# Meta scores by two matmuls a block instead of three, in a hybrid attention encoder on one core

## The chip, the cores and the metric

The kernel runs on one core of a Trainium2 chip. The metric is the device time of one execution in microseconds (us), lower is better. Inside the core five engines run side by side, each through its own instruction list in order: TensorE (PE in the profile, with PEld for its weight loads), VectorE (DVE), ScalarE (ACT), GpSimd (POOL) and SyncE (SP), which here issues all the DMA transfers. TensorE reads its operands from SBUF, the on-chip memory of 128 partitions, and writes to PSUM, a smaller memory that VectorE and ScalarE read.

## The reference

One encoder layer is applied to two token groups, 1024 prompt tokens and 256 sample tokens; each has 16 learned meta tokens put ahead of it. Cut to what matters:

```
u = rms_norm(h, norm_w) @ w_in                    # 2048 -> 6656, 52 strips of 128 columns
qa, ka, va, za, qb, kb, vb, zb = split(u)
# A heads (8, sharing 2 key/value heads): every query sees 16 meta keys and all real keys
s = q . k * 128**-0.5 ;  p = softmax(s) ;  o = p . v
# B heads (8): every query sees 16 meta keys and an 8x16 window of real keys, plus a position bias
s_meta = q . k_meta * scale
s_win  = q . k_win * scale + bias
p = softmax(concat(s_meta, s_win)) ; o = p_meta . v_meta + p_win . v_win
y = concat(o_a * silu(za), o_b * silu(zb)) @ w_out
return h + y                                       # real tokens only
```

All data is float32. The scores are large enough (the norm gains are scaled by 8) that the kernel keeps more than one rounded product: it splits an operand into a high part, rounded to the matmul's fast float32 kind (`F32R` in the code), and a low part, the rest, and sums high x high, high x low and low x high in PSUM. A plain float32 matmul needs no split and stands as two passes in the trace.

## The kernel before, in words

Tokens are processed in two chunks. Chunk 1 (0 to about 580 us) holds the sample tokens, the meta tokens and the first 240 prompt tokens; chunk 2 (to about 1800 us) the other 784 prompt tokens. In each chunk `strips` multiplies 128-column strips of `w_in` with the normalised tokens, 16 steps of three matmuls (L205 to L207) a strip and a block of up to 512 tokens. That stream of projection matmuls is most of the work of TensorE, and the attention blocks are laid between it. From about 1800 us on `outproj` (L946 to L948) makes the output.

An attention block covers 256 queries. There are 80 of them: 40 with all keys (`attend`; 8 sample blocks in chunk 1, 32 prompt blocks in chunk 2), 32 with windows (`attend_strip`, chunk 2 and the start of the output projection) and 8 sample blocks with windows (`attend_sample`, which makes its meta scores in one plain float32 matmul). A block runs: scores of the real keys (L328 to L330, or L434); scores of the meta keys; maximum over all keys (VectorE L278, then a reduction over partitions on GpSimd, L280); subtraction of it and exponentials; sums (L295, L297 on GpSimd); the product with the values (L368 to L370, or L466) and, in one more matmul, with the meta values (L371, L463); normalisation, gate and store (`put_y`).

The change concerns the meta scores of the 72 blocks of `attend` and `attend_strip`. The 16 meta keys stand three times side by side as 48 weight columns, so that the scores come out in three copies, on partitions 0 to 15, 16 to 31 and 32 to 47; `meta_probs` later turns the three into high, high and low parts of the probabilities (L285 to L290) for a single matmul with the meta values. `meta_scores` makes the scores with three matmuls of 256 query columns: high keys x high queries, high keys x low queries, low keys x high queries, all summed into the same 48 partitions of PSUM (L268 to L270); ScalarE then copies them, scaled, to the SBUF tile `Sm` (L272). The keys' tile `km` is built once per key head by `copy_km` (L500) or in `k_load` (L780, L781), and its two halves are handed on as a pair.

The order of the work is not written out. The kernel is traced in the order of the code, and a scheduler that carries estimated times lays out each engine's list. So an edit of one helper can move instructions far from it. SBUF is handed out by pools that are stacked one behind another: a tile that grows moves all that lie behind it. Each pool rotates a given number of buffers; `sp`, the PSUM pool of the scores, has two, `sm`, which holds `Sm`, has two.

Of the kernel before, what the change touches and what calls it, by code (L numbers as in the profile page):

```python
# [12 lines left out]
F32 = mybir.dt.float32  # L13
F32R = mybir.dt.float32r
AF = mybir.ActivationFunctionType
# [5 lines left out]
P = 128  # L21
DM = 2048
KT = 16
NMETA = 16
M3 = 3 * NMETA
NS = 256
NP = 1024
C1P = 240
# [10 lines left out]
QB = 256  # L39
# [11 lines left out]
class Kern:  # L51
# [212 lines left out]
    def meta_scores(self, pm, meta, qh, ql, scale):  # L264

        nc = self.nc
        kh, kl = meta
        nc.tensor.matmul(pm, kh, qh, start=True, stop=False)  # L268
        nc.tensor.matmul(pm, kh, ql, start=False, stop=False)
        nc.tensor.matmul(pm, kl, qh, start=False, stop=True)  # L270
        sm = self.sm.tile([M3, QB], F32, tag="Sm", name="Sm")
        nc.scalar.activation(sm[:], pm, AF.Copy, scale=scale)  # L272
        return sm

    def all_max(self, m1, sm):
# [41 lines left out]
    def attend(self, q, zs, keys, meta, vals, vmeta, ydst):  # L317

        nc = self.nc
        nt = len(keys)  # L320
        qh, ql = q[:, 0, :], q[:, 1, :]
        S = []
        mx = None
        for p in range(nt // 2):
            ps = self.sp.tile([P, 2, QB], F32, tag="sp", name="sp")
            for i in range(2):
                kh, kl = keys[2 * p + i]
                nc.tensor.matmul(ps[:, i, :], kh, qh, start=True, stop=False)  # L328
                nc.tensor.matmul(ps[:, i, :], kh, ql, start=False, stop=False)  # L329
                nc.tensor.matmul(ps[:, i, :], kl, qh, start=False, stop=True)  # L330
            s = self.s.tile([P, 2, QB], F32, tag="S", name="S")
            nc.scalar.copy(s[:], ps[:])  # L332
            S.append(s)
            if p == 1:
                mx = self.mx.tile([P, 2, QB], F32, tag="mx", name="mx")
                nc.vector.tensor_tensor(out=mx[:], in0=S[0][:], in1=ps[:], op=ALU.max)
            elif p > 1:
                nc.vector.tensor_tensor(out=mx[:], in0=mx[:], in1=ps[:], op=ALU.max)
        pm = self.sp.tile([P, 2, QB], F32, tag="sp", name="sm_ps")
        sm = self.meta_scores(pm[:M3, 0, :], meta, qh, ql, 1.0)  # L340
        src = S[0] if mx is None else mx
        m1 = self.t.tile([P, QB], F32, tag="t", name="m1")
        nc.vector.tensor_tensor(out=m1[:], in0=src[:, 0, :], in1=src[:, 1, :], op=ALU.max)
        ma = self.all_max(m1, sm)
        mb = ma[:].unsqueeze(1).to_broadcast([P, 2, QB])
        for p in range(nt // 2):
            s = S[p][:]
            nc.vector.tensor_tensor(out=s, in0=s, in1=mb, op=ALU.subtract)  # L348
            nc.scalar.activation(s, s, AF.Exp, scale=SCALE)
            if p == 1:  # L350
                acc = self.mx.tile([P, 2, QB], F32, tag="mx", name="acc")
                nc.vector.tensor_tensor(out=acc[:], in0=S[0][:], in1=S[1][:], op=ALU.add)
            elif p > 1:
                nc.vector.tensor_tensor(out=acc[:], in0=acc[:], in1=s, op=ALU.add)
        pm3 = self.meta_probs(sm, ma, SCALE)
        src = S[0] if nt == 2 else acc
        a1 = self.t.tile([P, QB], F32, tag="t", name="a1")
        nc.vector.tensor_tensor(out=a1[:], in0=src[:, 0, :], in1=src[:, 1, :], op=ALU.add)
        tot = self.all_sum(a1, sm)
        po = self.op.tile([P, QB], F32, tag="po", name="po")  # L360
        for j in range(nt):
            p, i = divmod(j, 2)
            if i == 0:
                ph = self.ph.tile([P, 2, QB], F32R, tag="ph", name="ph")
# [6 lines left out]
        nc.tensor.matmul(po[:], vmeta, pm3[:], start=False, stop=True)  # L371
        self.put_y(po, tot, zs, ydst)
# [39 lines left out]
    def attend_strip(self, q, qf, zs, k, meta, vals, vmeta, tab, w, ydst):  # L412

        nc = self.nc
        qv = q[:].rearrange("p i (g r) -> p i g r", g=4)[:, :, :, 64 * w:64 * w + 64]
        qfv = qf[:].rearrange("p (g r) -> p g r", g=4)[:, :, 64 * w:64 * w + 64]
        groups = {0: (0, 2), 3: (2, 4), 1: (0, 3), 2: (1, 4)}
        pa = self.sp.tile([P, 2, QB], F32, tag="sp", name="sp")  # L420
        pb = self.sp.tile([P, 2, QB], F32, tag="sp", name="sp")
        sa = self.s.tile([P, 2, QB], F32, tag="S", name="S")
        sb = self.s.tile([P, 2, QB], F32, tag="S", name="S")
        pa, pb, sa, sb = (x[:].rearrange("p a b -> p (a b)") for x in (pa, pb, sa, sb))

        def part(a, b, t):

            return (a[:, :P], b[:, :192], b[:, 192:384], a[:, P:2 * P])[t]

        for t in (0, 3, 1, 2):  # L430
            a, e = groups[t]
            dst = part(pa, pb, t)
            o = NMETA + 256 * t + 32 * WIN0[w]
            nc.tensor.matmul(dst, k[:, o:o + P], qfv[:, a:e, :], start=True, stop=True)  # L434
            if t == 3:
                sm = self.meta_scores(pa[:M3, 256:], meta, qv[:, 0], qv[:, 1], SCALE)
        ty = WTYPE[w]
        for x, y, n, o in ((sa, pa, 256, 64), (sb, pb, 384, 0)):
            nc.vector.scalar_tensor_tensor(out=x[:, :n], in0=y[:, :n], scalar=SCALE, in1=tab[:, ty, o:o + n],
                                           op0=ALU.mult, op1=ALU.add)  # L440
# [22 lines left out]
        nc.tensor.matmul(po[:], vmeta, pm3[:], start=True, stop=False)  # L463
        for t in (0, 3, 1, 2):
            a, e = groups[t]
            nc.tensor.matmul(po[:, 64 * a:64 * e], vals[:, t, :], part(sa, sb, t), start=False, stop=t == 2)  # L466
        self.put_y(po, tot, zs, ydst)
# [28 lines left out]

    def copy_km(self, k):

        km = self.k.tile([P, 2, 3, NMETA], F32R, tag="km", name="km")
        self.nc.scalar.copy(km[:], k.bitcast(F32).unsqueeze(2).to_broadcast([P, 2, 3, NMETA]))  # L500
        km = km[:].rearrange("p i c m -> p i (c m)")
        return km[:, 0], km[:, 1]

    def load_vm(self, g):

# [178 lines left out]
    def chunk2(self):  # L684
# [89 lines left out]
        def k_load(g):  # L774
            k = self.k.tile([P, NMETA + NP], F32, tag="k1", name="kfull")
            nc.sync.dma_start(k[:, :K0], self.kfd[g][:])
            nc.sync.dma_start(k[:, K0:], self.k2d[g][:])
            km = self.k.tile([P, 2, 3, NMETA], F32R, tag="km", name="km")
            full = k[:, :NMETA].unsqueeze(1).to_broadcast([P, 3, NMETA])
            nc.scalar.copy(km[:, 0], full)  # L780
            nc.vector.tensor_tensor(out=km[:, 1], in0=full, in1=km[:, 0].bitcast(F32), op=ALU.subtract)  # L781
            km = km[:].rearrange("p i c m -> p i (c m)")
            return k, (km[:, 0], km[:, 1])

        def q_load(h):
            qf = self.qf.tile([P, NP], F32, tag="qf", name="qfull")
# [416 lines left out]
```

## Time and profile before

| | |
|---|---|
| median of three runs | 2207.62 us (2204.06 to 2210.12) |
| the profiled execution | 2206.77 us, of which the span of the trace is 2204.7 us |
| TensorE busy in the span | 2180.8 us (99%), weight loads beside it 1964.3 us |
| VectorE, ScalarE, GpSimd busy | 1634.2, 1115.5 and 525.2 us |
| granted TensorE clock | 0.999 of full speed over the span |
| the 216 meta-score matmuls | 72 each on L268, L269 and L270 |

In the rows of the profile, a group reads: line, engine, operation, output tile <- input tiles, shape, count, then busy time and mean duration, then idle time of the engine before it and what ended it. A row such as `128*48 128x256` is a matmul with 48 weight columns and 256 streamed columns. Matmuls overlap in the pipeline, so the duration of one (280 ns) is longer than the distance from its start to the start of the next; the cost of one in a full stream is that distance. Times in a row of a waits view are us in total, number of times, longest.

### The profile page before, as it was taken

Reading aid. Unit: us, or ns where it says so; the run is one execution under the profiler, and the core shown is the slowest. Engines: PE = TensorE matmul, PEld = TensorE weight load, DVE = VectorE, ACT = ScalarE, POOL = GpSimd, SP = SyncE. Lnnn points to the kernel's source line nnn. Section 1 sums busy time; section 2 is a strip of 40 time slices with the busy share of each in tenths; the row PEclk is TensorE's granted clock in tenths of the full one; section 3 lists DMA queues with packets and bytes.
Section 4 is the critical chain, followed back from the end, with each engine's and each line's share of the span. In section 5 each row is a group of like instructions: output and inputs, shape, how many; then the busy total and the mean of one; then the engine's idle time right before and its main releaser. Section 6 shows DMA issues by size and latency. Waiting matters only on the chain.

```text
span 2204.7 us, 36270 instructions
## 1 busy us (share of the span) xinstructions
PE 2180.8 (99%) x12816; PEld 1964.3 (89%) x12816; DVE 1634.2 (74%) x2895; ACT 1115.5 (51%) x2272; POOL 525.2 (24%) x249
## 2 busy tenths in 40 slices
PE   8999999999999999999999999999999999999999
PEld 7888788888878999999999999998889889999999
DVE  7687876787764989976899989767768777536743
ACT  6555444455454666755666756444444454222220
POOL 1232421132211332221233223423423312000000
PEclk9999999999999999999999999999999999999999
DMA  8767889989464333334333335644433464745663
GB/s 291 224 191 226 268 287 309 331 271 291 135 214 146 107 111 115 102 110 142 101 107 111 105 121 161 184 144 133 126 114 115 136 225 151 234 136 163 212 205 112
DMA packets 264533, 383.96 MB, mean 174 GB/s; under 512 B 45824, under 2 KB 120224, under 8 KB 264352
## 3 DMA queue, kind: packets, MB, share of 16 engines
q1 hardware_dynamic: 264352, 381.66, 54.5%
q8 instruction: 100, 1.64, 0.3%
q14 instruction: 81, 0.66, 0.1%
HBM read 281.01 MB, written 100.38 MB: 173 GB/s over the span
## 4 chain that ended last, share of the span: by engine, by line
PE 89%; DVE 5%; DMA 3%; issue 1%; ACT 1%; POOL 0%; SPq 0%; DVEq 0%; POOLq 0%; ACTq 0%
PE pp L205 20%; PE pp L207 20%; PE pp L206 19%; PE pq L947 6%; PE pq L948 6%; PE pq L946 6%; PE po L466 2%; PE sp L330 1%; PE sp L328 1%; PE sp L329 1%; PE po L368 1%; PE po L369 1%; PE po L370 1%; PE sp L434 1%; DMA wr<-in_w_in 1%
## 5 line engine op out<-in xcount | busy, mean ns | idle before, releaser
L205 PE MATMUL pp<-x,wh 128*128 128x512 f32 (+1 forms) x2496 | 895.2, 360 | 8.7 <-ACT wh L57 7.2
L207 PE MATMUL pp<-x,wl 128*128 128x512 f32 (+1 forms) x2496 | 890.6, 357 | 0.0
L206 PE MATMUL pp<-x,wh 128*128 128x512 f32 (+1 forms) x2496 | 889.1, 356 | 0.2 <-DVE x L155 0.2
L205 PEld LDWEIGHTS pp<-x,wh 128*128 128x128 f32 x2496 | 469.2, 188 | 72.7 <-ACT wh L57 8.5
L206 PEld LDWEIGHTS pp<-x,wh 128*128 128x128 f32 x2496 | 470.5, 188 | 60.8 <-DVE x L155 0.9
L207 PEld LDWEIGHTS pp<-x,wl 128*128 128x128 f32 x2496 | 469.1, 188 | 61.9 <-DVE wl L58 0.7
L58 DVE TENSOR_TENSOR wl<-wr,wh 128x512 fp32r<-128x512 f32 (+1 forms) x402 | 303.8, 768 | 139.2 <-ACT wh L57 86.5
L57 ACT CAST wh<-wr 128x512 fp32r<-128x512 f32 (+1 forms) x402 | 240.1, 611 | 237.7 <-PE pp L206 169.3
L215 POOL PARTITION_ALL_REDUCE m<-ms x78 | 228.9, 2934 | 410.1 <-ACT ms L213 371.0
L297 POOL PARTITION_ALL_REDUCE tot<-a x80 | 178.8, 2234 | 454.6 <-DVE a L295 431.2
L947 PE MATMUL pq<-ym,wh 128*128 128x320 f32 x896 | 276.9, 309 | 1.9 <-DVE ym L58 1.9
L948 PE MATMUL pq<-ym,wl 128*128 128x320 f32 x896 | 276.8, 309 | 0.7 <-DVE wl L58 0.7
L946 PE MATMUL pq<-ym,wh 128*128 128x320 f32 x896 | 276.2, 309 | 1.1 <-ACT ym L57 1.1
L280 POOL PARTITION_ALL_REDUCE ma<-m x80 | 108.1, 1351 | 420.7 <-DVE m L278 417.1
L947 PEld LDWEIGHTS pq<-ym,wh 128*128 128x128 f32 x896 | 168.1, 188 | 2.6 <-DVE ym L58 2.6
L946 PEld LDWEIGHTS pq<-ym,wh 128*128 128x128 f32 x896 | 168.0, 188 | 1.7 <-ACT ym L57 1.7
L948 PEld LDWEIGHTS pq<-ym,wl 128*128 128x128 f32 x896 | 168.1, 188 | 1.0 <-DVE wl L58 0.9
L190 ACT CAST wh<-wr 128x512 fp32r<-128x512 f32 x132 | 81.6, 618 | 52.7 <-PE pp L206 49.6
L332 ACT COPY S<-sp 128x512 f32<-128x512 f32 x136 | 78.5, 582 | 56.3 <-PE sp L330 51.3
L64 ACT ACTIVATE rs_l<-m 128x512 f32<-128x512 f32 (+1 forms) x78 | 43.9, 563 | 124.1 <-DVE m L216 119.4
L348 DVE TENSOR_TENSOR S<-S,ma 128x512 f32<-128x512 f32 x136 | 98.4, 779 | 9.2 <-POOL ma L280 9.2
L58 DVE TENSOR_TENSOR pl<-S,ph 128x512 fp32r<-128x512 f32 x136 | 97.3, 727 | 9.9 <-ACT ph L57 9.2
(201 smaller groups left out, 3185.9 us busy)
## 6 DMA issues: line engine op xcount, KB each, us to landing
wr<-in_w_in SPq DMA_DIRECT2D x414, 256.0 KB, 3.8
wld<-wl SPq DMA_DIRECT2D x132, 256.0 KB, 4.6
wl<-wld SPq DMA_DIRECT2D x132, 256.0 KB, 3.3
wq<-in_w_out SPq DMA_DIRECT2D x64, 256.0 KB, 5.5
td<-wq SPq DMA_DIRECT2D x64, 256.0 KB, 4.6
wr<-td SPq DMA_DIRECT2D x64, 256.0 KB, 3.4
yr<-yd SPq DMA_DIRECT2D x48, 320.0 KB, 4.1
wr<-in_w_out SPq DMA_DIRECT2D x48, 256.0 KB, 3.8
```

The source lines that it names most:

```text
L57: self.hi = nc.scalar.copy(hi, full).ins
L58: return nc.vector.tensor_tensor(out=lo, in0=full, in1=hi.bitcast(F32), op=ALU.subtract).ins
L205: nc.tensor.matmul(p[:, :n], wh[:, k, :], xh[:, :n], start=first, stop=False)
L206: nc.tensor.matmul(p[:, :n], wh[:, k, :], xl[:, :n], start=False, stop=False)
L207: nc.tensor.matmul(p[:, :n], wl[:, k, :], xh[:, :n], start=False, stop=last)
L215: nc.gpsimd.partition_all_reduce(m2[:], ms[:], P, RED.add)
L280: nc.gpsimd.partition_all_reduce(ma[:], m1[:], P, RED.max)
L297: nc.gpsimd.partition_all_reduce(tot[:], a1[:], P, RED.add)
L348: nc.vector.tensor_tensor(out=s, in0=s, in1=mb, op=ALU.subtract)
L946: nc.tensor.matmul(ps[:, b, :B], wh, yh[:, o], start=k == 0, stop=False)
L947: nc.tensor.matmul(ps[:, b, :B], wh, yl[:, o], start=False, stop=False)
L948: nc.tensor.matmul(ps[:, b, :B], wl, yh[:, o], start=False, stop=k == 7)
```

## The change

`meta_scores` runs two matmuls instead of three. The weight columns are now the 16 high meta keys four times and the 16 low ones three times, 112 columns in one tile. One matmul streams the high queries and one the low queries, summed in the same 112 partitions of PSUM. Partitions 0 to 47 then hold high keys x (high + low queries), partitions 64 to 111 low keys x (high + low queries); the fourth copy of the high keys only fills the columns up to 64. ScalarE copies the low half, scaled, to a new SBUF tile `Sl`, and VectorE scales the high half and adds `Sl` into `Sm`. The product low x low, left out before, is now included.

```
-        kh, kl = meta
-        nc.tensor.matmul(pm, kh, qh, start=True, stop=False)
-        nc.tensor.matmul(pm, kh, ql, start=False, stop=False)
-        nc.tensor.matmul(pm, kl, qh, start=False, stop=True)
-        sm = self.sm.tile([M3, QB], F32, tag="Sm", name="Sm")
-        nc.scalar.activation(sm[:], pm, AF.Copy, scale=scale)
+        nc.tensor.matmul(pm[:ML + M3], meta, qh, start=True, stop=False)
+        nc.tensor.matmul(pm[:ML + M3], meta, ql, start=False, stop=True)
+        sm, sl = (self.sm.tile([M3, QB], F32, tag=n, name=n) for n in ("Sm", "Sl"))
+        nc.scalar.activation(sl[:], pm[ML:ML + M3], AF.Copy, scale=scale)
+        nc.vector.scalar_tensor_tensor(out=sm[:], in0=pm[:M3], scalar=scale, in1=sl[:], op0=ALU.mult, op1=ALU.add)
...
     def copy_km(self, k):
-        km = self.k.tile([P, 2, 3, NMETA], F32R, tag="km", name="km")
-        self.nc.scalar.copy(km[:], k.bitcast(F32).unsqueeze(2).to_broadcast([P, 2, 3, NMETA]))
-        km = km[:].rearrange("p i c m -> p i (c m)")
-        return km[:, 0], km[:, 1]
+        km = self.k.tile([P, 7, NMETA], F32R, tag="km", name="km")
+        for i, c, n in ((0, 0, 4), (1, 4, 3)):
+            self.nc.scalar.copy(km[:, c:c + n], k[:, i, :].bitcast(F32).unsqueeze(1).to_broadcast([P, n, NMETA]))
+        return km[:].rearrange("p c m -> p (c m)")
...
-            km = self.k.tile([P, 2, 3, NMETA], F32R, tag="km", name="km")
-            full = k[:, :NMETA].unsqueeze(1).to_broadcast([P, 3, NMETA])
-            nc.scalar.copy(km[:, 0], full)
-            nc.vector.tensor_tensor(out=km[:, 1], in0=full, in1=km[:, 0].bitcast(F32), op=ALU.subtract)
+            km = self.k.tile([P, 7, NMETA], F32R, tag="km", name="km")
+            full = [k[:, :NMETA].unsqueeze(1).to_broadcast([P, n, NMETA]) for n in (4, 3)]
+            nc.scalar.copy(km[:, :4], full[0])
+            nc.vector.tensor_tensor(out=km[:, 4:], in0=full[1], in1=km[:, :3].bitcast(F32), op=ALU.subtract)
```

A new constant, `ML = 4 * NMETA`, shifts the line numbers between it and `meta_scores` by one (L205 to L207 become L206 to L208); from L276 on they are as before.

Two things follow in the built program. First, places in SBUF. `km` grows from 384 to 448 bytes a partition, and `Sl` adds two buffers of 1024 bytes. The tiles stacked behind `km` start 64 bytes later, and those behind the `sm` pool 2112 bytes later. In chunk 2 the queries `q` go from byte 53120 to 53184, `ph` from 75648 to 75712, the first `S` from 65408 to 65472. All operands that the attention's matmuls stream (`q`, `qs`, `qfull`, `S`, `ph`, `pl`) started at a multiple of 128 bytes and now start 64 bytes past one. The streamed operands of the projections (`x`, `ym`) and the meta probabilities `Pm` keep their places.

Second, the order. In the sixth full block of chunk 2, the list of TensorE (PE) held the three meta matmuls (`sm_ps`) behind the first products with the values (`po`) of the block before:

```order
L368 MATMUL po<-ph,va 128x256
L369 MATMUL po<-ph,va 128x256
L268 MATMUL sm_ps<-q,km 48x256
L269 MATMUL sm_ps<-q,km 48x256
L270 MATMUL sm_ps<-q,km 48x256
L206 MATMUL pp<-x,wh 128x272
L207 MATMUL pp<-x,wl 128x272
L205 MATMUL pp<-x,wh 128x512
```

Of the change, the same place in the list of TensorE:

```order
L206 MATMUL pp<-x,wh 128x512
L207 MATMUL pp<-x,wh 128x512
L268 MATMUL sm_ps<-q,km 112x256
L269 MATMUL sm_ps<-q,km 112x256
L208 MATMUL pp<-x,wl 128x512
L206 MATMUL pp<-x,wh 128x272
L207 MATMUL pp<-x,wh 128x272
L208 MATMUL pp<-x,wl 128x272
```

The pair now stands between projection matmuls, and the products with the values follow a few rows later.

For the same block VectorE (DVE) had, before, the last maximum of the real keys (`mx`), then the gate work of a strip (`za`), the maximum over the two halves (`m`), the meta scores' share in it (L278), and the end of an earlier block:

```order
L338 TENSOR_TENSOR mx<-mx,sp 128x512
L259 TENSOR_SCALAR za<-z,za 128x512
L259 TENSOR_SCALAR za<-z,za 128x272
L343 TENSOR_TENSOR m_8594<-mx 128x256
L278 TENSOR_TENSOR m_8594<-m_8594,Sm 16x256
L313 TENSOR_TENSOR y<-po,z 128x256
L306 TENSOR_TENSOR tot<-tot,r 128x256
L307 TENSOR_SCALAR r<-tot,r 128x256
L314 TENSOR_SCALAR y<-y,r 128x256
```

Of the change, VectorE at the same block:

```order
L338 TENSOR_TENSOR mx<-mx,sp 128x512
L255 TENSOR_TENSOR z<-pp,rb_359 128x512
L272 TENSOR_SCALAR Sm<-sm_ps,Sl 48x256
L343 TENSOR_TENSOR m_8611<-mx 128x256
L255 TENSOR_TENSOR z<-pp,rb_359 128x272
L306 TENSOR_TENSOR tot<-tot,r 128x256
L278 TENSOR_TENSOR m_8611<-m_8611,Sm 16x256
L307 TENSOR_SCALAR r<-tot,r 128x256
L260 TENSOR_SCALAR za<-z,za 128x512
L313 TENSOR_TENSOR y<-po,z 128x256
```

The new add (L272) stands ahead of the maximum, and other work of the scheduler's choice was laid around it. The count of rows changes by 72 fewer matmuls on TensorE, 72 more adds on VectorE and two more copies on ScalarE; no DMA is added or taken away, though the places of some in the list of SP move.

More of the change, by code (lines that the diff above doesn't have):

```diff
@@ L25 @@
 M3 = 3 * NMETA
+ML = 4 * NMETA
 NS = 256
@@ L339, in attend @@
         pm = self.sp.tile([P, 2, QB], F32, tag="sp", name="sm_ps")
-        sm = self.meta_scores(pm[:M3, 0, :], meta, qh, ql, 1.0)
+        sm = self.meta_scores(pm[:, 0, :], meta, qh, ql, 1.0)
         src = S[0] if mx is None else mx
@@ L435, in attend_strip @@
             if t == 3:
-                sm = self.meta_scores(pa[:M3, 256:], meta, qv[:, 0], qv[:, 1], SCALE)
+                sm = self.meta_scores(pa[:, 256:], meta, qv[:, 0], qv[:, 1], SCALE)
         ty = WTYPE[w]
@@ L777, in k_load @@
             nc.sync.dma_start(k[:, K0:], self.k2d[g][:])
-            km = self.k.tile([P, 2, 3, NMETA], F32R, tag="km", name="km")
-            full = k[:, :NMETA].unsqueeze(1).to_broadcast([P, 3, NMETA])
-            nc.scalar.copy(km[:, 0], full)
-            nc.vector.tensor_tensor(out=km[:, 1], in0=full, in1=km[:, 0].bitcast(F32), op=ALU.subtract)
-            km = km[:].rearrange("p i c m -> p i (c m)")
-            return k, (km[:, 0], km[:, 1])
+            km = self.k.tile([P, 7, NMETA], F32R, tag="km", name="km")
+            full = [k[:, :NMETA].unsqueeze(1).to_broadcast([P, n, NMETA]) for n in (4, 3)]
+            nc.scalar.copy(km[:, :4], full[0])
+            nc.vector.tensor_tensor(out=km[:, 4:], in0=full[1], in1=km[:, :3].bitcast(F32), op=ALU.subtract)
+            return k, km[:].rearrange("p c m -> p (c m)")
         def q_load(h):
```

## Prediction

> **What bounds the kernel now.** I read the page's engine totals and its chain of work first, then the table of stages, then the waits of TensorE.
>
> ```profile
> span 2204.7 us, 36270 instructions
> ...
> PE 2180.8 (99%) x12816; PEld 1964.3 (89%) x12816; DVE 1634.2 (74%) x2895; ACT 1115.5 (51%) x2272; POOL 525.2 (24%) x249
> ...
> PE 89%; DVE 5%; DMA 3%; issue 1%; ACT 1%; POOL 0%; SPq 0%; DVEq 0%; POOLq 0%; ACTq 0%
> ```
>
> TensorE is busy 2180.8 of 2204.7 us and carries 89% of the chain that ends last. The rest, 24 us, is all that it ever stands idle. The stage with the 32 full blocks of chunk 2 (700 to 1345 us) shows it at its purest; columns are the stretch, its length, then busy us and count of each engine, granted clock, DMA share and GB/s:
>
> ```profile
> 700.00:1345.00 645.00, 645.00 (x4188) 590.13 (x4187) 553.06 (x999) 425.25 (x872) 185.22 (x91) 1.00 0.37 112
> ```
>
> PE has no idle time there, at the full clock; VectorE, second, is at 553.06 / 645 = 86%, and DMA at 37%. What TensorE does wait for, over the whole span:
>
> ```profile
> PE pp L205 <- ACT wh L57: 7.2, 2, 5.4
> PE sp L328 <- ACT qs L57: 2.4, 2, 1.3
> ...
> PE po L463 <- DVE Pm L290: 1.4, 1, 1.4
> ...
> PE po L371 <- DVE Pm L290: 1.1, 3, 0.5
> ```
>
> The largest is the start-up (5.4 us at once). The attention chain, from meta scores to meta probabilities `Pm`, holds TensorE back 1.4 + 1.1 = 2.5 us in all 72 blocks. So a matmul taken out of the stream is worth its place in the stream, and a longer chain behind it is worth little as long as that cover holds.
>
> **The matmul removed.** Its price is the distance between starts, read from the list of TensorE in time order (start, duration, instruction):
>
> ```profile
> 715.14 0.29 PE L205 MATMUL pp<-x,wh 128*128 128x272 f32 x1
> 715.26 0.28 PE L206 MATMUL pp<-x,wh 128*128 128x272 f32 x1
> 715.39 0.29 PE L207 MATMUL pp<-x,wl 128*128 128x272 f32 x1
> 715.51 0.28 PE L268 MATMUL sm_ps<-q,km 128*48 128x256 f32 x1
> 715.63 0.28 PE L269 MATMUL sm_ps<-q,km 128*48 128x256 f32 x1
> 715.75 0.28 PE L270 MATMUL sm_ps<-q,km 128*48 128x256 f32 x1
> 715.87 0.39 PE L205 MATMUL pp<-x,wh 128*128 128x512 f32 x1
> 716.09 0.39 PE L206 MATMUL pp<-x,wh 128*128 128x512 f32 x1
> 716.32 0.39 PE L207 MATMUL pp<-x,wl 128*128 128x512 f32 x1
> 716.55 0.28 PE L205 MATMUL pp<-x,wh 128*128 128x272 f32 x1
> 716.67 0.28 PE L328 MATMUL sp<-q,kf 128*128 128x256 f32 x1
> ...
> 717.25 0.28 PE L330 MATMUL sp<-q,kf 128*128 128x256 f32 x1
> 717.37 0.28 PE L206 MATMUL pp<-x,wh 128*128 128x272 f32 x1
> ```
>
> The three meta matmuls take 715.87 - 715.51 = 0.36 us, 0.12 each; the six of L328 to L330 take 717.37 - 716.67 = 0.70 us, 0.117 each. These have 128 weight columns where the meta matmuls have 48, and stream the same 256 columns: the price hangs on the streamed columns, not on the weights. So going from 48 to 112 columns costs nothing on this engine. Their weight loads differ, but lie beside the matmul before:
>
> ```profile
> L330 PEld LDWEIGHTS sp<-q,kf 128*128 128x128 f32 x256 | 48.1, 188 | 0.1
> ...
> L270 PEld LDWEIGHTS sm_ps<-q,km x32: 120/121/123, 715.6 to 1337.3; 128*48 128x48 f32 x32
> L270 PE MATMUL sm_ps<-q,km x32: 274/280/285, 715.7 to 1337.4; 128*48 128x256 f32 x32
> ...
> L270 PE MATMUL sp<-q,km x32: 276/279/285, 1344.3 to 1828.9; 128*48 128x256 f32 x32
> ...
> L270 PE MATMUL sm_ps<-qs,km x8: 276/280/283, 87.9 to 266.3; 128*48 128x256 f32 x8
> ```
>
> 32 + 32 + 8 = 72 matmuls leave, 72 x 0.118 = **8.5 us less**, all of it on the path, since TensorE is the bound in every stage in which they stand.
>
> **The work added.** ScalarE's copy of 48x256 from PSUM stays, with `Sl` as its target, at the same price (first two rows). VectorE gains an operation of 48 partitions by 256 with one PSUM and one SBUF input. Nearest are the window scores' scaled add (third row, the same operation and inputs) and the gate's product (fourth); the fifth has both inputs in SBUF:
>
> ```profile
> L272 ACT ACTIVATE Sm<-sm_ps x40: 361/376/384, 88.5 to 1338.3; 48x256 f32<-48x256 f32 x40
> L272 ACT ACTIVATE Sm<-sp x32: 360/378/380, 1344.9 to 1832.6; 48x256 f32<-48x256 f32 x32
> ...
> L439 DVE SCALAR_TENSOR_TENSOR S<-sp,bt 128x256 f32<-128x256 f32 x32 | 13.4, 417 | 5.2 <-ACT Sm L272 4.9
> ...
> L310 DVE TENSOR_TENSOR y<-po,z 128x256 f32<-128x256 f32 x32 | 13.4, 419 | 8.3 <-PE po L466 8.3
> ...
> L285 DVE TENSOR_TENSOR Sm<-Sm,ma x80: 404/410/2464, 96.4 to 1848.8; 48x256 f32<-48x256 f32 x80
> ```
>
> All sit at 0.42 us a piece: 72 x 0.42 = 30.2 us more on VectorE, of which 32 x 0.42 = 13.4 us fall into the stage 700 to 1345 us (86% becomes 88%). That is cover that stays. The add waits for ScalarE's copy, and behind it on VectorE wait the maximum (L278), GpSimd's reduction and so the exponentials: the chain of a block grows by 0.42 us plus whatever stands between in the list. The PSUM buffer of the scores is also given back one operation later; no wait of TensorE on a free `sp` buffer is in the list above, so I cost that at nothing. What the longer chain costs TensorE is bounded by the two rows on `Pm`: nothing where the scheduler lays the last matmul a little later, 2.5 us where those waits come twice as often. I take 1.5 us. Below nothing too: up to 2.5 us if the new order removes them.
>
> **Two copies.** `copy_km` runs two copies where it ran one, four times in all, and ScalarE's 51% hides them: under 4 x 0.3 us by its own rows of 274 ns:
>
> ```profile
> L500 ACT CAST km<-kc x2: 273/274/274, 56.6 to 166.8; 128x96 fp32r<-128x96 f32 x2
> ```
>
> No DMA is added. SP's list is shifted in places; the stages with these blocks have DMA at 37% (above), so I cost that at nothing.
>
> **The sum.** 2206.8 (the profiled execution) - 8.5 + 1.5 = **2199.8, say 2200 us**. That execution lies 0.9 us under the median of the three runs. A measurement of this kernel can tell about 0.3% from no change, so faster begins at 2201.0 and slower at 2214.2: the gain, 0.35%, is only just beyond that. The mechanism's own range is 2195 (the `Pm` waits gone) to 2205.
>
> **Rival B: the 64-byte shift prices the streamed reads.** All streamed operands of the attention move from a multiple of 128 bytes to 64 past one. No row before has such an operand, so the price is bounded. From the rows above a streamed column costs (0.227 - 0.117) / 256 = 0.43 ns, with 0.227 = (716.55 - 715.87) / 3. One more piece of 64 bytes (16 columns) at each start would cost 7 ns, one of 128 bytes 14 ns. The counts that stream moved operands:
>
> ```profile
> L328 PE MATMUL sp<-q,kf x256: 276/280/363, 704.3 to 1336.2; 128*128 128x256 f32 x128
> ...
> L328 PE MATMUL sp<-qs,kc x16: 274/282/385, 87.0 to 265.8; 128*128 128x256 f32 x16
> ...
> L466 PE MATMUL po<-S,vw x256: 270/300/328, 1367.8 to 1856.1; 128*128 128x128 f32 x64, 128*128 128x192 f32 x64
> ```
>
> Three lines of scores and three of products with 256 + 16 each, 144 meta matmuls, and two lines of 256 float32 passes (L434 is as L466): 6 x 272 + 144 + 512 = 2288. At 7 ns that is 16.0 us, and the time 2199.8 + 16.0 = **2216 us, slower**; at 14 ns 2232. It takes the whole gain from 3.1 ns a matmul on (8.5 - 1.5 = 7.0 us over 2288) and makes the kernel slower by 0.3% from 6.3 ns on (2214.2 - 2199.8 = 14.4 us over 2288). For it: nothing but that every streamed operand so far happens to be aligned, so the trace can't deny it. Against it: ends that don't fall on 128 bytes are not rounded up. 272 columns are 8.5 pieces of 128 bytes and take (715.51 - 715.14) / 3 = 0.123 us, on the straight line between 256 and 512 (0.124), not the 0.131 of 9 pieces. And the streamed data of L205 is never moved. [...]
>
> **Rival C: VectorE's added time comes through.** VectorE stands at 86% in the stage with the full blocks; if its 14% of idle time is only waiting that can't be filled, the 13.4 us added there reach the end: 2206.8 - 8.5 + 13.4 = **2212 us**. It decides from the point at which the `wl` and `pl` subtractions (L58), queued behind the add, come later than the matmul that reads them. For it: 72 adds stand ahead of the reduction that starts the second half of each block, and the whole order is laid anew. Against it: TensorE has no idle at all in that stage, and the rows on `Pm` show four short waits.
>
> **Chances.** The forecast has 0.47, B 0.35, C 0.18. Of the forecast's 0.47, 0.27 lie under 2201.0, 0.19 above it within 0.3%, and 0.01 beyond; of B 0.28 are slower, 0.05 within, 0.02 faster (a small price and fewer waits); C divides evenly, 0.09 and 0.09. Together faster 0.29, same 0.33, slower 0.38. The range runs from 2194, just under the forecast's own, to 2222, B at 10 ns a matmul; what is left out is B at over 10 ns, about 0.12, and some 0.06 at both ends.
>
> **What the profile after would show.** Right: 72 fewer matmuls, meta pairs 0.24 us apart in the stream, L328 and L368 still 0.117 us apart, TensorE's busy time down by about 8.5 us, waits on `Pm` under 5 us, the add at 0.42 us. B: the distances of L328 to L330, L368 to L370 and L434, L466 longer by the same few ns, those of L205 and L946 not. C: unchanged distances, but idle time of TensorE ended by VectorE (`pl`, `Pm`, `wl`). Wrong in another way: an idle stretch at the change of chunks (580 to 700 us) or at the start, from the new order alone.

## The result and the profile after

| | before | after |
|---|---|---|
| median (range) | 2207.62 us (2204.06 to 2211.79) | 2200.85 us (2199.17 to 2204.62) |
| profiled execution | 2206.77 us | 2202.31 us |
| span of the trace | 2204.7 us | 2200.5 us |

The ratio after to before is 0.9971, with a 95% interval from 0.9962 to 0.9980. The kernel became faster by 6.8 us, and by the bound of 0.3% this is just at the edge between faster and the same. The time forecast was 2200.0 us.

The page of the changed kernel has, as engine totals and as shares of the chain that ended last:

```profile
span 2200.5 us, 36174 instructions
...
PE 2174.5 (99%) x12744; PEld 1960.0 (89%) x12744; DVE 1648.5 (75%) x2967; ACT 1120.6 (51%) x2276; POOL 518.8 (24%) x249
...
PE 91%; DMA 3%; DVE 3%; SPq 1%; ACT 1%; issue 1%; POOL 0%; DVEq 0%; POOLq 0%; ACTq 0%
```

TensorE has 12816 - 12744 = 72 matmuls fewer, VectorE 72 operations more. ScalarE runs four copies more (x2276 against x2272), two for each of the two kinds of `km` that `copy_km` makes, where the section on the change counts two in all. TensorE's busy time fell by 6.3 us. The stage with the full blocks, in the same view as before:

```profile
700.00:1345.00 645.00, 645.00 (x4173) 590.10 (x4172) 561.84 (x1035) 429.38 (x877) 183.92 (x91) 1.00 0.37 113
```

VectorE rose from 553.06 to 561.84 us of 645, to 87%, and TensorE has no idle time there still. A group of the real keys' scores, and a meta pair with the projection matmul behind it, in time order:

```profile
708.61 0.28 PE L328 MATMUL sp<-q,kf 128*128 128x256 f32 x1
708.73 0.28 PE L329 MATMUL sp<-q,kf 128*128 128x256 f32 x1
708.85 0.28 PE L330 MATMUL sp<-q,kf 128*128 128x256 f32 x1
708.96 0.28 PE L328 MATMUL sp<-q,kf 128*128 128x256 f32 x1
...
714.32 0.28 PE L268 MATMUL sm_ps<-q,km 128*112 128x256 f32 x1
714.43 0.28 PE L269 MATMUL sm_ps<-q,km 128*112 128x256 f32 x1
714.55 0.40 PE L206 MATMUL pp<-x,wh 128*128 128x512 f32 x1
```

The pair takes 714.55 - 714.32 = 0.23 us, the old three took 0.36; 112 weight columns cost no more place in the stream than 48. The scores of the real keys, which now stream from an address 64 bytes past a multiple of 128, still follow each other at (708.96 - 708.61) / 3 = 0.117 us. The lines of the added and the changed operations (duration minimum, median and maximum in ns):

```profile
L268 PEld LDWEIGHTS sm_ps<-q,km x32: 174/174/175, 714.2 to 1332.9; 128*112 128x112 f32 x32
...
L271 ACT ACTIVATE Sl<-sm_ps x40: 380/381/383, 89.3 to 1334.5; 48x256 f32<-48x256 f32 x40
...
L272 DVE SCALAR_TENSOR_TENSOR Sm<-sm_ps,Sl x40: 402/409/418, 89.8 to 1337.4; 48x256 f32<-48x256 f32 x40
```

The add costs 0.41 us, as its neighbours did. What TensorE waits for, over the span:

```profile
PE pp L206 <- ACT wh L58: 7.5, 2, 5.6
PE pq L945 <- ACT ym L58: 5.0, 3, 3.8
...
PE po L371 <- DVE Pm L290: 1.0, 2, 0.8
...
PE po L463 <- DVE Pm L290: 0.2, 1, 0.2
```

The waits on `Pm` fell from 2.5 to 1.2 us. New is the second row of this view: at one place the output projection waits 3.8 us for its operand `ym`.

**Where the gain goes.** To place the difference I set the start of the n-th projection matmul (`pp`, then `pq`) of one trace against that of the other; between the two stands the same work of the projections. After minus before:

| matmul that starts before at | 617 us | 1332 us | 1522 us | 1700 us | 1790 us | 1872 us | 2168 us |
|---|---|---|---|---|---|---|---|
| after - before, us | -1.1 | -4.1 | -6.2 | -9.8 | -9.0 | -4.2 | -4.2 |

Up to 1790 us the gain is 9.0 us. It grows over the stages that hold the blocks; single points swing by some us where a block is laid a little earlier or later. Some 1.5 us of the 9.0 come at one place near 1590 us, where the kernel before waits 1.4 us on `Pm` (the prediction's row of L463) and the changed one 0.2. Then, between 1790 and 1872 us, 4.8 us are handed back at one place, and nothing changes after it. The chain of waits of the changed kernel at that place, in order of time (start, duration, what):

```profile
1856.05 5.46 DMA ym<-yd
1861.50 0.02 issue
1861.53 0.73 ACT ym L58
1862.26 0.02 issue
1862.28 0.84 DVE ym L59
1863.12 0.04 issue
1863.16 0.42 PE pq L946
1863.59 0.27 PE pq L947
...
1867.46 0.15 PE pq L945
```

This is the hand-over from the attention to the output projection. The strip n = 8 of `outproj` is the first that needs the output of the last attention block (head 15), as its eighth operand, k = 7. That block stores its output to DRAM (`yd`), the output projection loads it (`ym`, 5.46 us), ScalarE and VectorE split it, and only then can TensorE go on. The stores and the load in SyncE's queue, of the changed kernel:

```profile
1834.13 0.39 SPq L315 DMA_DIRECT2D yd<-y  x1
1843.43 0.38 SPq L315 DMA_DIRECT2D yd<-y  x1
1852.56 0.37 SPq L315 DMA_DIRECT2D yd<-y  x1
1856.05 0.38 SPq L880 DMA_DIRECT2D ym<-yd  x1
```

And of the kernel before:

```profile
1838.42 0.38 SPq L315 DMA_DIRECT2D yd<-y  x1
1848.10 0.38 SPq L315 DMA_DIRECT2D yd<-y  x1
1857.39 0.38 SPq L315 DMA_DIRECT2D yd<-y  x1
1861.29 0.32 SPq L881 DMA_DIRECT2D ym<-yd  x1
```

The last three blocks end 9.1 to 9.7 us apart in both kernels, and the load follows the last store by 3.5 and 3.9 us. But the last block ends only 4.8 us earlier (1857.39 - 1852.56), while TensorE arrives 9.0 us earlier. So TensorE, which waited 1.1 us there before, now waits 3.8. The wait costs more than itself: behind it the matmuls stand 0.27 us apart where they stand 0.15 apart from 1867 us on. The stages of the changed kernel around it (the third number from the end of a row is the granted clock):

```profile
1858.00:1863.00 5.00, 0.92 (x5) 0.43 (x3) 1.87 (x3) 0.72 (x1) 0.00 (x0) 1.00 0.60 227
1863.00:1867.00 4.00, 3.84 (x15) 3.84 (x16) 1.67 (x3) 0.72 (x2) 0.00 (x0) 0.57 0.16 63
1867.00:1875.00 8.00, 8.00 (x57) 8.00 (x56) 4.32 (x6) 1.69 (x5) 0.00 (x0) 1.00 0.71 227
```

After the idle stretch the clock is granted at 0.57, and 15 matmuls run in 4 us instead of about 28 (57 in 8 us); summed over the slow ones this is 1.6 us beyond the wait.

### The profile page after: what moved, and what is told of

Read it like the earlier page. It is cut to its first block, busy times and chain, and to the rows that moved or that the text cites. A ratio compares the mean times of both kernels' runs of the same rounds, so it can differ in the third digit from the quotient of the medians.

```text
span 2200.5 us, 36174 instructions
## 1 busy us (share of the span) xinstructions
PE 2174.5 (99%) x12744; PEld 1960.0 (89%) x12744; DVE 1648.5 (75%) x2967; ACT 1120.6 (51%) x2276; POOL 518.8 (24%) x249
## 4 chain that ended last, share of the span: by engine, by line
PE 91%; DMA 3%; DVE 3%; SPq 1%; ACT 1%; issue 1%; POOL 0%; DVEq 0%; POOLq 0%; ACTq 0%
PE pp L206 20%; PE pp L208 20%; PE pp L207 20%; PE pq L946 6%; PE pq L947 6%; PE pq L945 6%; PE po L466 1%; PE po L368 1%; PE sp L434 1%; PE po L370 1%; PE sp L328 1%; PE po L369 1%; PE sp L330 1%; PE sp L329 1%; DMA wld<-wl 1%
## 5 line engine op out<-in xcount | busy, mean ns | idle before, releaser
L206 PE MATMUL pp<-x,wh 128*128 128x512 f32 (+1 forms) x2496 | 895.5, 360 | 8.8 <-ACT wh L58 7.5
L208 PE MATMUL pp<-x,wl 128*128 128x512 f32 (+1 forms) x2496 | 891.3, 357 | 0.0
L207 PE MATMUL pp<-x,wh 128*128 128x512 f32 (+1 forms) x2496 | 888.9, 356 | 0.4 <-DVE x L156 0.4
L206 PEld LDWEIGHTS pp<-x,wh 128*128 128x128 f32 x2496 | 469.6, 188 | 73.4 <-ACT wh L58 8.5
L207 PEld LDWEIGHTS pp<-x,wh 128*128 128x128 f32 x2496 | 470.6, 189 | 61.8 <-DVE x L156 1.1
L208 PEld LDWEIGHTS pp<-x,wl 128*128 128x128 f32 x2496 | 469.4, 188 | 62.1 <-DVE wl L59 0.6
L59 DVE TENSOR_TENSOR wl<-wr,wh 128x512 fp32r<-128x512 f32 (+1 forms) x402 | 299.2, 756 | 156.7 <-ACT wh L58 119.6
L945 PE MATMUL pq<-ym,wh 128*128 128x320 f32 x896 | 277.4, 310 | 5.0 <-ACT ym L58 5.0
L947 PE MATMUL pq<-ym,wl 128*128 128x320 f32 x896 | 277.4, 310 | 0.2 <-DVE wl L59 0.2
L945 PEld LDWEIGHTS pq<-ym,wh 128*128 128x128 f32 x896 | 168.8, 189 | 6.1 <-ACT ym L58 5.9
L947 PEld LDWEIGHTS pq<-ym,wl 128*128 128x128 f32 x896 | 168.8, 188 | 0.5 <-DVE wl L59 0.5
L59 DVE TENSOR_TENSOR pl<-S,ph 128x512 fp32r<-128x512 f32 x136 | 96.1, 719 | 10.8 <-ACT ph L58 10.5
L349 ACT ACTIVATE S<-S 128x512 f32<-128x512 f32 x136 | 84.0, 629 | 34.1 <-DVE S L348 34.1
```

What stands on the lines that cost most here:

```text
L59: return nc.vector.tensor_tensor(out=lo, in0=full, in1=hi.bitcast(F32), op=ALU.subtract).ins
L206: nc.tensor.matmul(p[:, :n], wh[:, k, :], xh[:, :n], start=first, stop=False)
L207: nc.tensor.matmul(p[:, :n], wh[:, k, :], xl[:, :n], start=False, stop=False)
L208: nc.tensor.matmul(p[:, :n], wl[:, k, :], xh[:, :n], start=False, stop=last)
L945: nc.tensor.matmul(ps[:, b, :B], wh, yh[:, o], start=k == 0, stop=False)
L947: nc.tensor.matmul(ps[:, b, :B], wl, yh[:, o], start=False, stop=k == 7)
```

## The experiments

The theory: a matmul is worth its place in TensorE's stream, 0.118 us each, so 8.5 us; the add lies beside other work; and what is missing of the gain is lost at the hand-over, where the last block's chain is late. Two rivals are those of the prediction: B, the shift by 64 bytes has a price and hides a gain; C, VectorE's added time comes through. A third came with the result: the loss at the hand-over belongs to a single execution. Kernels that were run together share the runs of the kernel before. Its medians were 2210.60 us (for the first four rows), 2208.45 us (the next four) and 2208.24 us (the last three).

| kernel | median us | ratio to before (95% interval) |
|---|---|---|
| `before_shift` | 2210.08 | 1.0001 (0.9991 to 1.0011) |
| `after_aligned` | 2202.56 | 0.9963 (0.9949 to 0.9976) |
| `after_again` | 2203.28 | 0.9964 (0.9951 to 0.9976) |
| `early_blocks` | 2203.38 | 0.9968 (0.9956 to 0.9981) |
| `after_late7` | 2195.15 | 0.9942 (0.9929 to 0.9956) |
| `before_late7` | 2206.82 | 0.9990 (0.9981 to 0.9999) |
| `three_wide` | 2218.58 | 1.0047 (1.0034 to 1.0060) |
| `add_twice` | 2203.42 | 0.9971 (0.9961 to 0.9982) |
| `late7_again` | 2196.73 | 0.9954 (0.9941 to 0.9968) |
| `three_late7` | 2211.34 | 1.0013 (1.0004 to 1.0022) |
| `pair_late7` | 2201.67 | 0.9967 (0.9955 to 0.9978) |

**The shift by 64 bytes, alone (`before_shift`).** The kernel before, with `km` made 64 bytes longer: the streamed operands of the attention move, the order stays the same.

```
-        km = self.k.tile([P, 2, 3, NMETA], F32R, tag="km", name="km")
+        km = self.k.tile([P, 7, NMETA], F32R, tag="km", name="km")[:, :6].rearrange("p (i c) m -> p i c m", i=2)
```

> The kernel before with the tile km padded from 384 to 448 bytes a partition and nothing else: every list of instructions stays as it was, and the streamed operands of the attention start 64 bytes past a multiple of 128, as in the changed kernel. If the shift costs nothing: 2207.6 us within 3, and L328 to L330 and L368 to L370 keep 0.117 to 0.119 us from start to start. Rival B (a shifted start is paid): 7 ns on 2288 matmuls, 2224 us; at 3 ns 2214 us.

Measured: 1.0001, up to 1.0011 at the interval's end. That end is 2.4 us over the prediction's 2288 matmuls plus the 72 of the third meta line, 1 ns each, where B asked for 7. Its stage of full blocks reads as that of before, with 4185 matmul records for 4188 and no idle time to speak of:

```profile
700.00:1345.00 645.00, 644.92 (x4185) 590.35 (x4184) 552.75 (x998) 423.98 (x871) 184.36 (x91) 1.00 0.37 112
```

From 695 to 1329 us, where some 1600 of the moved operands are streamed, its projection matmuls shift against those of before by 0.1 us in all. One row of this trace matters further down. Near 1590 us it waits longer on `Pm` than the kernel before (2.9 us for 1.4), though every engine runs the same operations on the same tiles in the same order:

```profile
PE po L463 <- DVE Pm L290: 2.9, 1, 2.9
```

**The shift undone (`after_aligned`).** The changed kernel with `km` made 512 bytes, so that the streamed operands start at multiples of 128 again:

```
-        km = self.k.tile([P, 7, NMETA], F32R, tag="km", name="km")
+        km = self.k.tile([P, 8, NMETA], F32R, tag="km", name="km")[:, :7]
```

> The changed kernel with km padded to 512 bytes, so that the streamed operands start at multiples of 128 bytes again; the lists of instructions stay those of the changed kernel. If the shift costs nothing: as the changed kernel, 2201 us within 3. Rival B: what the shift took comes back, 2185 us at 7 ns a matmul.

Measured: 0.9963 against 0.9964 of the changed kernel as it stands, on the same chip (`after_again`), and from 695 to 1329 us no shift of the projection matmuls over 0.1 us. B falls from both sides.

**The changed kernel on another chip (`after_again`).** No edit.

> The changed kernel once more, for a second profile. In the first, TensorE waited 3.8 us once in the output projection (L945, on the load of the last attention output), which the kernel before did not. If that wait belongs to the new order of the lists, it comes again, 3 us or more; if it was a slow transfer of one execution, it stays under 1.5 us and the span is 2197. Median 2201 us within 2 either way.

The wait at the hand-over is there again, as it is in `after_aligned` (4.0 us) and `early_blocks` (4.1 us); the third rival falls, and the loss belongs to the order. The row of the wait:

```profile
PE pq L945 <- ACT ym L58: 4.6, 3, 3.9
```

The same comparison by projection matmuls gives -11.0 us at 1790 us and -4.4 us at the end. This trace is 2.1 us ahead of the first one of the changed kernel by 20 us already, from the start-up.

**More blocks earlier (`early_blocks`).** In `outproj` the window blocks that are left are drawn two per strip instead of one, to end the last block earlier:

```
                 next(self.blocks, None)
+                next(self.blocks, None)
```

> The changed kernel with the last four window blocks issued two behind each of the first two products of the output projection, not one behind each of the first four, so that the last attention output is stored some 14 us earlier. If the wait on its load is a hand-over that comes too late for the shorter stream: the 3.8 us go, 2197 to 2198 us. If the wait only shows another limit: no change, 2201 us. Blocks crowded together may wait on their own chain of VectorE and GpSimd: 2203 us.

This was a miss: the wait stayed at 4.1 us. The edit moved nothing: in the trace every engine runs the same operations on the same tiles in the same order as in the changed kernel, and the last three stores are 9.3 and 9.1 us apart as there. So the run does not test what an earlier end of the last block would give, and whether the pace of 9 us is set by the order, by the reduction on GpSimd or by VectorE stays open.

**The late operand used last (`after_late7`, `before_late7`).** Whatever paces the last block, TensorE can do other work until it has ended. Strips 8 and 9 run their first seven operands, and then the eighth of both:

```
-            ps = self.products(ws.pop(n), [ys[8 * (n // 8) + k] for k in range(8)])
+            yk = [ys[8 * (n // 8) + k] for k in range(8)]
+            if n == 8:
+                p8, p9 = (self.products(ws[i], yk, range(7)) for i in (8, 9))
+                ps = self.products(ws.pop(8), yk, (7,), p8)
+            elif n == 9:
+                ps = self.products(ws.pop(9), yk, (7,), p9)
+            else:
+                ps = self.products(ws.pop(n), yk)
```

`products` takes the operands `ks` and a PSUM tile to go on with. Of the changed kernel:

> The changed kernel, with the first two steps of the output projection that need the last attention output (n = 8 and 9) doing their products with the other seven heads first and that one at their end; same matmuls, same sums in another order. TensorE then comes to the last output some 6 us later. If the 3.8 to 4.1 us wait there is gain handed back at a hand-over: the wait goes and the time falls by about 4 us, to 2199 us on the chip where the changed kernel had 2203. If the time does not fall, the end is held by something else.

Of the kernel before:

> The same reordering in the kernel before, which waited 1.1 us there. Hand-over theory: 1 us less, 2209.5 us where the kernel before has 2210.6, and so 8.5 to 10.5 us between this and after_late7, the whole price of 72 matmuls. If the reordering helps by itself, it falls by 4 us too and the distance stays 7 us.

Measured: 2195.15 and 2206.82 us. The reordered changed kernel lies 13.3 us under the kernel before on its chip, where the changed one lies 6.8 and 7.3 us under it on theirs: the edit gives it 6.0 to 6.5 us, and the kernel before 1.6 us. The projection matmuls show that this comes at the hand-over: between 1850 and 1900 us `after_late7` gains 6.0 us on the changed kernel, `before_late7` 1.1 us on the kernel before. The edit changes only who uses the late operand when, and the changed kernel gains more by it: what was lost there was the hand-over. Repeated on another chip:

> The reordered kernel as it was run before, for comparison on this chip. If the gain from taking head 15 last belongs to the list: 13 us under the kernel before (ratio 0.994), no wait over 1.2 us on L945 to L947, granted clock 1.00 from 1850 to 1870 us. If it was that one run: a ratio of 0.9965 or more, and the hand-over wait of 3 us or more back.

2196.73 us, 11.5 us under the kernel before, so that the edit is worth 4.2 us at the least and 6.5 at the most by the medians, and again 6.0 us at the hand-over in its trace. The load of the last output starts within 0.2 us of that in the changed kernel, and the clock stays at full:

```profile
1855.89 0.38 SPq L880 DMA_DIRECT2D ym<-yd  x1
```

```profile
1858.00:1863.00 5.00, 5.00 (x36) 5.00 (x36) 1.74 (x3) 0.73 (x1) 0.00 (x0) 1.00 0.68 256
1863.00:1867.00 4.00, 3.97 (x27) 3.70 (x27) 1.52 (x3) 0.00 (x0) 0.00 (x0) 1.00 0.02 4
```

In these 9 us TensorE is busy for 8.97 us, in the changed kernel for 0.92 + 3.84 = 4.76. This version beats both kernels, the one before by 11.5 and 13.3 us.

The two reordered kernels lie 2206.82 - 2195.15 = 11.7 us apart, more than the 8.5 to 10.5 expected. In the trace of `before_late7` one cause is a wait of TensorE that the kernel before has at 1.4 us and the changed one at 0.2, followed by a slow stretch of the clock (1.8 us beyond the wait):

```profile
PE po L463 <- DVE Pm L290: 2.9, 1, 2.9
```

```profile
1592.00:1594.00 2.00, 2.00 (x8) 1.81 (x7) 1.31 (x4) 2.00 (x6) 0.44 (x1) 0.50 0.10 22
```

The reordering did not make this wait: up to there the order is that of the kernel before, and `before_shift` waits 2.9 us at the same place. So this order has the wait at 1.4 or 2.9 us from one execution to the next, where all six traces with the order of the changed kernel have 0.2, and so have the two with a third matmul put back (below). It is a part of the measured gain that belongs to the new order and not to the matmuls.

**A third matmul put back (`three_wide`, `three_late7`).** The changed kernel, and the reordered one, with a third matmul of 112 columns in every pair, so that the low queries count twice:

```
         nc.tensor.matmul(pm[:ML + M3], meta, qh, start=True, stop=False)
+        nc.tensor.matmul(pm[:ML + M3], meta, ql, start=False, stop=False)
         nc.tensor.matmul(pm[:ML + M3], meta, ql, start=False, stop=True)
```

> The changed kernel with a third matmul of 112 columns in each of the 72 blocks: the one with the low queries runs twice, so their part counts double in the meta scores. As many matmuls as before, with the add on VectorE. Stream theory: 72 x 0.118 = 8.5 us more than the changed kernel if all of it is on the path, 4.5 to 8.5 with the 4 us of the hand-over wait, so 2207 to 2212 us where the changed kernel has 2203. If the gain came from the new order of the lists and not from the matmul: 2203 us, no change.

> The reordered kernel with a third meta matmul of 112 columns (the low queries are counted twice, so the scores differ from the reference). Theory: a matmul costs its place, 72 x 0.12 = 8.6 us, and what three_wide cost beyond that was the hand-over and waits in chunk 1 from an order laid anew; with the hand-over out of the way 8.6 us plus 0 to 5 us, 2204 to 2209 us, and in the full blocks of chunk 2 (700 to 1330 us) 0.12 us a block, 3.8 us. Rival: a 112-column matmul in this place costs more than its place (a dearer weight load, or a PSUM buffer held longer), 0.2 us a matmul: 14 us or more, and over 6 us in the full blocks of chunk 2.

Both came out dearer than expected: `three_wide` 1.0047, some 17 us above the changed kernel (10.1 us over the kernel before, where that one lies 7 under it), and `three_late7` 14.6 us above `late7_again` (2211.34 - 2196.73; 13.0 by the ratios). By the medians alone the rival of the second (0.2 us a matmul) would stand. The projection matmuls decide otherwise:

| matmul that starts in the base at | 105 us | 313 us | 695 us | 1329 us | 1691 us | 1782 us | 1825 us | 2157 us |
|---|---|---|---|---|---|---|---|---|
| `three_late7` - `late7_again`, us | 0.1 | 5.2 | 5.0 | 8.9 | 11.7 | 12.3 | 13.7 | 13.7 |
| `pair_late7` - `late7_again`, us | 1.7 | 4.0 | 1.5 | 1.7 | 6.9 | 5.5 | 6.0 | 6.1 |

From 695 to 1329 us, with 31 of the blocks and no idle time of TensorE in either kernel, the third matmul costs 8.9 - 5.0 = 3.9 us, 0.13 each; `three_wide` has 9.7 - 5.8 = 3.9 there against the changed kernel. That is close to the theory's number (31 x 0.118 = 3.7), where the rival needs over 6. Most of the rest lies in chunk 1: the eight blocks up to 313 us account for 1 us of the 5.2, the other 4 are waits, which both traces with this order have. Another 1.3 us come near 1790 us. TensorE's largest waits from 20 to 330 us of `three_late7` are on values (`vt`) and queries (`qs`) and on nothing of the meta scores:

```profile
PE tp L249 <- DVE vt L242: 3.0, 2, 1.6
PE sp L329 <- ACT qs L58: 1.9, 3, 1.3
```

against these of `late7_again` in the same stretch:

```profile
PE po L368 <- ACT ph L58: 2.2, 3, 1.6
PE po L371 <- DVE Pm L290: 1.4, 4, 0.8
PE tp L249 <- DVE vt L242: 0.3, 1, 0.3
```

**The add twice, and the add left out (`add_twice`, `pair_late7`).** Once the same add runs a second time with the same result; once, in the reordered kernel, it and the low half are left out and ScalarE copies the high half to `Sm`.

```
         nc.vector.scalar_tensor_tensor(out=sm[:], in0=pm[:M3], scalar=scale, in1=sl[:], op0=ALU.mult, op1=ALU.add)
+        nc.vector.scalar_tensor_tensor(out=sm[:], in0=pm[:M3], scalar=scale, in1=sl[:], op0=ALU.mult, op1=ALU.add)
```

> The changed kernel with the add of the two halves run twice on VectorE, the same result. 30 us more work on VectorE, and a chain longer by 0.42 us in each block. Forecast: hidden, 0 to 1.5 us over the changed kernel, 2203 to 2205 us. Rival C (VectorE's time in the stage of the full blocks comes through): 13 us more, 2216 us.

```
-        sm, sl = (self.sm.tile([M3, QB], F32, tag=n, name=n) for n in ("Sm", "Sl"))
-        nc.scalar.activation(sl[:], pm[ML:ML + M3], AF.Copy, scale=scale)
-        nc.vector.scalar_tensor_tensor(out=sm[:], in0=pm[:M3], scalar=scale, in1=sl[:], op0=ALU.mult, op1=ALU.add)
+        sm = self.sm.tile([M3, QB], F32, tag="Sm", name="Sm")
+        nc.scalar.activation(sm[:], pm[:M3], AF.Copy, scale=scale)
```

> The reordered kernel with the two meta matmuls, but without VectorE's add: ScalarE copies the high half to Sm and the low half is left out (low keys x queries are missing from the scores). Theory: the add lies beside TensorE's work and costs nothing; within 2.5 us of the reordered kernel (the waits on Pm and the order laid anew), VectorE's busy time down by 72 x 0.41 = 30 us. Rival C: VectorE's added time comes through; the full blocks of chunk 2 alone give back up to 13 us, 5 us or more in all.

`add_twice` has the ratio of the changed kernel, 0.9971, with 27 us more on VectorE (1675.5 us). Inside, two things cancel: it is 6.4 us later at 1750 us, 3.9 of that by 695 us, and then has no long wait at the hand-over, where it gets 5 us back. So its time was as expected by luck. In the stage of the full blocks the second add is not free: there this kernel falls 2.7 us behind the changed one (at matmuls with the same attention work behind them), and TensorE stands idle for 1.1 us:

```profile
700.00:1345.00 645.00, 643.90 (x4157) 588.02 (x4156) 570.63 (x1058) 423.69 (x874) 182.35 (x91) 1.00 0.38 112
```

VectorE is at 570.63 / 645 = 88% there. How much of the 2.7 us is the add and how much the order laid anew isn't shown, so how much more VectorE could take stays open. `pair_late7` tests the first add. It missed its expected 2.5 us on the side that no theory had: 2201.67 us, 5 us slower without the add than with it (2.9 by the ratios, whose intervals overlap). In the stage of the full blocks (700 to 1328 us; first the reordered kernel, then the one without the add) nothing moved:

```profile
700.00:1328.00 628.00, 628.00 (x4066) 574.92 (x4064) 545.45 (x1004) 417.90 (x853) 178.15 (x88) 1.00 0.37 112
```

```profile
700.00:1328.00 628.00, 628.00 (x4063) 574.74 (x4062) 531.52 (x973) 413.50 (x852) 180.88 (x88) 1.00 0.37 112
```

VectorE does 13.9 us less, TensorE is without idle time in both, and the projection matmuls shift by 1.7 - 1.5 = 0.2 us. C falls for this stage: the one add of the change costs nothing there. The 5 us come from elsewhere: 1.5 us up to 695 us, all of it there by 105 us, and most of the rest at one wait on `Pm` near 1587 us, with the slow clock behind it, that the trace without the add has and the other has not:

```profile
PE po L462 <- DVE Pm L289: 1.9, 1, 1.9
```

```profile
1590.20:1592.20 2.00, 2.00 (x8) 1.72 (x7) 1.93 (x4) 1.17 (x4) 1.87 (x1) 0.50 0.40 111
```

What stays open: no experiment moves the order without an edit to the work, so that the cost of an order laid anew isn't predicted by anything here. Nor is each difference between two single traces the order's: executions of one order differ as well, by 2.1 us in the start-up between the two traces of the changed kernel and by 4.3 us near 1590 us between `before_shift` and the kernel before. The stage without idle time, the hand-over, whose wait stands in all four traces with the order of the changed kernel and the late operand in its old place, and the medians bear the weight here.

## Why the prediction was right, point by point

- **72 x 0.118 = 8.5 us, all on the path:** held as a distance of starts, and roughly as a price. 112 columns cost no more place than 48. Put back, a matmul cost 3.9 us for 31 blocks in the clean stage, 0.13 each; taken out, it gave less there: the changed kernel gains 4.1 - 1.2 = 2.9 us on the kernel before from 695 to 1329 us, 0.09 each, and the same in `after_again`. One thing on the other side is seen, not explained: the projection matmuls of 512 columns start 231.4 ns after one another on average in this stage where they took 230.8, some 0.8 us over 1250 of them. The 9.0 us gained by 1790 us are so near to 8.5 in part by luck, with some 1.5 us from the wait near 1590 us. "All of it on the path, since TensorE is the bound in every stage in which they stand" failed in the consequence: the prediction asked what holds TensorE in those stages, and not what TensorE would run into behind them. TensorE's busy time fell by 6.3 us, not 8.5: the 1.6 us of slow matmuls behind the new wait are in it.
- **+1.5 us for the chain of `Pm`:** the term was put in the wrong place. The waits on `Pm` fell by 1.3 us, within its lower bound of -2.5, though the add does stand in the chain. What cost time was the other wait behind the same chain, the hand-over of the last block: 4.8 us. Against the profiled execution after, 2202.31 us, the sum of 2199.8 is 2.5 us low: 4.8 us missing and 1.5 + 1.3 = 2.8 us too much make 2.0 of it, and the other 0.5 isn't resolved. The median of after lies 1.5 us under that execution, so the forecast looks closer than its account was. A price that was about right and a wrong account of the loss gave a right time; that it came so near was luck.
- **SyncE's list and the queue of `ym`, costed at nothing:** this step looked at the DMA share in the stages with the blocks. The trace of before showed that TensorE already stood still for the last head's operand (1800 to 1875 us, its waits):

```profile
PE pq L947 <- DVE ym L58: 1.1, 1, 1.1
```

8.5 us taken ahead of it had to lengthen that wait unless the last block came earlier too. "Wrong in another way" named the start and the change of chunks as places for such an idle stretch, and not this one.
- **B, the 64-byte shift, at 0.35:** refuted from both sides, 1.0001 (0.9991 to 1.0011) with the shift alone and 0.9963 against 0.9964 with the shift undone. The runs show it for starts 64 bytes past a multiple of 128 and for no others. The evidence that the prediction had against B (ends that are not rounded up, 0.123 us for 272 columns) deserved more weight than it got, and with less on B the chances would not have leaned to slower.
- **C, VectorE, at 0.18:** refuted in the stage that it named, 0.2 us for 13.9 us of VectorE's work. With a second add the stage was 2.7 us longer, so how far this cover reaches stays open.
- **Add 0.42 us, copies hidden, 112 columns free:** the add took 0.41 us, `Sl` 0.38 us as `Sm` before, the weight load of 112 columns 174 ns beside the matmul ahead.
- **The range of 2194 to 2222** held the time; its upper part was there for B.

## What to carry to other kernels

When TensorE is the bound, a matmul taken out is worth about the distance of starts (here 0.118 us, and 0.09 to 0.13 measured in the stage without idle time), but only up to the next hand-over that something else paces: look in the trace of before for the last short wait behind the edited stages, and ask whether its producer comes earlier by as much as TensorE does. Where it doesn't, lay work that doesn't need the late operand ahead of it; here this gave 4 to 6 us, nearly as much as the change itself. Where a scheduler lays the order anew at each edit, a kernel carries some us of luck of its order, and a single trace some of its execution (here 2.1 and 4.3 us): take a second trace of the same order, and compare the same instruction in two traces, stage by stage, before a median is put down to the edit.

## What was not expected of the hardware

A wait of TensorE can cost more than its length. After 3.8 us of waiting at the hand-over the granted clock was 0.57 over the next 4 us, and the slow matmuls added 1.6 us; after the waits of 2.9 and 1.9 us near 1590 us (`before_late7`, `pair_late7`) it was 0.50 over 2 us, and they added 1.5 to 1.8 us. In the changed kernel it was back at 1.00 from 1867 us on, in `before_late7` from 1594 us on. The length of the wait alone doesn't decide it. In the profiled execution of `late7_again` TensorE waited 2.1 us at one place (L249, on `vm`), and the granted clock was 1.0 over the whole span. And with one and the same order it stayed at 1.00 from 1778 to 1790 us in the changed kernel, with waits of 1.1 and 0.9 us in that stretch, while in `after_again` the matmuls of L945 to L947 stood 0.27 us apart from 1785.2 to 1787.6 us, where those of the changed kernel stand 0.15 apart. What does decide it, no run here shows.

A streamed operand of TensorE that starts 64 bytes past a multiple of 128 has no price that could be measured: 1 ns a matmul at the most by the medians, and 0.1 us over some 1600 of them in the stage of the full blocks.
